# Attention of a decoder trunk: both key groups' scores in one step on alternating row halves, and sums over values with the values as weights

## The chip, the cores and the metric

The kernel runs on one core of a Trainium2 chip. The metric is the device time of one launch in microseconds, the median of several runs. A core has five engines with queues of their own: TensorE (PE in the profile, with its weight loads as PEld), VectorE (DVE), ScalarE (ACT), GpSimdE (POOL), and SyncE (SP), which here only issues DMAs.

## What is computed

One step of a two-layer decoder on 304 columns: 16 learned tokens and 256 prompt tokens (columns 0 to 271, the prompt group) and 8 sequences of 4 new tokens (columns 272 to 303, the sample group). Per layer:

```python
proj = x @ w_in                      # q: 8 heads x 64, k, v: 2 key heads x 64; xr, gate, g_attn, g_lru: 1024 each
s = einsum(q, k) * HEAD_DIM ** -0.5  # window of 128 keys, masked with NEG_INF
m = maximum(s.max(-1), sink)
p = exp(s - m)
denom = p.sum(-1) + exp(sink - m)    # a learned sink of each head joins the sum
attn = einsum(p / denom, v)
rec = rg_lru(causal_conv(xr)) * gelu(gate)
mix = (sigmoid(g_attn) * (attn @ w_attn_proj) + sigmoid(g_lru) * (rec @ w_lru_proj)) @ w_out
x = layer_norm(alpha * x + mix)
x = layer_norm(alpha * x + swiglu(x))
```

All results are float32. The eight query heads share two key heads: heads 0 to 3 belong to group 0, heads 4 to 7 to group 1.

## The kernel before, in words

Columns are tokens, rows are channels, so that the result of a product is the moving operand of the next. Every large product is three float32r products of split parts (`wh`, `wl` are the two parts of a weight unit, `xh`, `xl` those of the activations): L363, L364 and L365, 24 of them for one tile of 128 output columns. Such a tile is one job, and a weight unit of eight 128 x 128 tiles feeds it. ACT and DVE split the weights (L212, L213) up to four units ahead.

The jobs of the first half of a layer are counted as steps: the q and k products up to step 6, then `ga`, `xr`, the rest of `ga`, `gate` and `gl`, up to step 37. The attention and the recurrence have no stretch of their own. A table `PLAN` names for each layer the step at which a piece of them is written into the program, between jobs or in the middle of one: `a0` and `ad` the first step and the spacing of attention steps, `c0` and `g0` those of the convolution and of the gates (`rg`), `r` the square roots, `p0` and `m0` the scan and what follows it. A scheduler then sets the order on each engine.

The attention of the prompt group has three blocks of queries: block 0, the 16 learned tokens (layer 0 only); block 1, the next 128 tokens, with 16 + 128 keys; block 2, the last 128, with 128 + 128 keys. A `Unit` is one block, one group `g` and two heads (four in block 0). So layer 0 has 2 + 4 + 4 units, layer 1 has 4 + 4; one `Sample` unit stands among them. A unit goes through four stages, some attention steps apart (`BEHIND`):

- `scores`: the mask goes into a bank `sc` as a bf16 product (L514), the products of q (weights, 64 rows: rows 0 to 63 for group 0, 64 to 127 for group 1) and keys add to it (L518), DVE takes the maximum (L522, L523), ACT the exponentials with their sums (L528) into `P`.
- `turn`: TensorE transposes `P`, key block by key block (L541), into `pt`, and ACT copies it to `PT` (L544, L547).
- `values`: for each head and key block a product with `PT` as weights (16 or 128 rows) and 64 columns of the values `vn` moving (L558) into a bank `o` of the whole block. After the block's last unit DVE divides by the denominators (L563 to L568) into `O`.
- `back`: `O` is transposed back (L580, `ot`) and split into `ath` and `atl` (L350, L351), which the products with `w_attn_proj` (`ap`) read after step 37.

`v_turn` brings the values into rows of keys at step 8 (L480 to L482). Tiles come from 51 slots and PSUM tiles from 8 banks, each in rotation, with their users' ends as the only waits. A float32 product shows in the trace as two records, each with a weight load of its own.

Of the kernel before, what the change touches and what calls it, by code (L numbers as in the profile page):

```python
# [35 lines left out]
    dict(a0=10, ad=1, c0=14, cd=1, g0=18, gd=0.75, r=23.5, p0=29.5, pd=1, m0=33.5, sx=21.5, vt=8),  # L36
    dict(a0=12, ad=1.75, c0=13.5, cd=1.5, g0=16.5, gd=1.25, r=26, p0=26, pd=2.25, m0=30, sx=9, vt=8),
# [4 lines left out]
NC = 2  # L42
HOOK = 4
BEHIND = ((0, 2, 3, 4), (0, 2, 4, 6))
# [14 lines left out]
def ffn_order():  # L59
    """The inner layer's pairs of columns, and the parts of its way back, each LAG pairs behind its last one."""  # L60
    order, due = [], {min(b + LAG, 22): (a, b) for a, b in FPARTS}
    for f in range(2, 23):
        if f in due:
            order.append(due[f])
        if f < 22:
            order.append(f)
    return order


def unit_list():  # L70
    """The units of 128 x 128 weight tiles in the order in which TensorE takes them."""
# [51 lines left out]
def trunk_kernel(ctx, tc, I, O):  # L123
# [100 lines left out]
    def ahead(u):  # L224
        """Split the units that come up to LA main units behind u."""
# [102 lines left out]
    class Split:  # L328
        """Activations as pairs of tiles, each in two float32r parts, which take their place when first used."""
# [16 lines left out]
    def split(parts, x, scale=None):  # L346
        """parts = x (times a scale of each row), in two parts that float32r holds."""
# [8 lines left out]
    def product(ps, n, u, i0, ks, xs, cs, start=True, stop=True):  # L356
        """ps[:, :n] += the tiles of unit u from i0 on, times those of xs."""
# [31 lines left out]
    def job(name, n, src, cs, ks=range(8), fills=()):  # L389
        """The product of one tile of columns; fills come between its halves."""  # L390
# [10 lines left out]
    def grouped(name, cols, src, between=None):  # L401
        """The products of four tiles of columns, with the contraction's tiles on the outside."""
# [21 lines left out]
    for l in range(DEPTH):  # L424
# [10 lines left out]
        vn = slot(nm("vn"), [128, 4, 128])  # L435
# [3 lines left out]
        def unfold(ps, n, ccs, out=None):  # L439
            """The product, with the spread and the shift of the LayerNorm before it."""  # L440
# [34 lines left out]
        def v_turn():  # L475
# [7 lines left out]
            pool.dma_start(O["wvp"][l], vn[:, 2, :])  # L483
            pool.dma_start(O["wvn"][l], vn[:32, 3, :])
# [4 lines left out]
        V0, V1, V2, VN = (vn[:, j, :] for j in range(4))  # L489
        BLK = {  # L490
            0: dict(q0=0, nq=16, keys=(0, 16), mask=mask0, v=((V0, 16),)),
            1: dict(q0=16, nq=128, keys=(0, 144), mask=mask1, v=((V0, 16), (V1, 128))),
            2: dict(q0=144, nq=128, keys=(16, 272), mask=mask2, v=((V1, 128), (V2, 128))),
        }
        blk_state = {}

        class Unit:
            """Scores of some heads of a block, from the products to the sum over the values."""

            def __init__(self, b, g, ts):  # L500
                self.b, self.g, self.ts = b, g, ts

            def scores(self):
                B = BLK[self.b]
                nq, (k0, k1), nt = B["nq"], B["keys"], len(self.ts)
                nk = k1 - k0
                if self.b not in blk_state:
                    blk_state[self.b] = dict(
                        nm=tiny("nm", 8), rs=tiny("rs", 8), left=8)
                S = blk_state[self.b]  # L510
                ps = bank(nm("sc"))
                w = 512 // nt
                p3 = ps[:nq, :].rearrange("p (a b) -> p a b", a=nt)[:, :, :nk]
                pe.matmul(p3, identb[:nq, :nq], B["mask"][:nq, None, :].to_broadcast([nq, nt, nk]),  # L514
                          start=True, stop=False, skip_group_check=True)
                gs = slice(64 * self.g, 64 * self.g + 64)
                for a, t in enumerate(self.ts):
                    pe.matmul(p3[:, a, :], qr[t // 2][gs, t % 2, B["q0"]:B["q0"] + nq], kr[gs, k0:k1],  # L518
                              start=False, stop=True, skip_group_check=True)
                c = slice(4 * self.g + self.ts[0], 4 * self.g + self.ts[0] + nt)  # L520
                mx = tiny("mx", 8)
                dve.tensor_reduce(mx[:nq, :nt], p3, axis=AX.X, op=OP.max)  # L522
                dve.scalar_tensor_tensor(S["nm"][:nq, c], mx[:nq, :nt], -0.125, nsink[:nq, l, c],  # L523
                                         op0=OP.mult, op1=OP.min)
                self.P = slot(nm("P"), [128, nt, nk])
                for a in range(nt):
                    h = c.start + a
                    act.activation(self.P[:nq, a, :], p3[:, a, :], AF.Exp, bias=S["nm"][:nq, h:h + 1],  # L528
                                   scale=0.125, accum_out=S["rs"][:nq, h:h + 1])

            def turn(self):
                B = BLK[self.b]
                nq, nt = B["nq"], len(self.ts)
                p = bank(nm("pt"))
                nv = len(B["v"])
                p4 = p[:, :nt * nv * nq].rearrange("p (a b c) -> p a b c", a=nv, b=nt)
                self.PT = slot(nm("PT"), [128, nv, nt, nq])
                for a in range(nt):
                    o = 0
                    for j, (_, n) in enumerate(B["v"]):  # L540
                        pe.transpose(p4[:n, j, a, :], self.P[:nq, a, o:o + n], identf[:nq, :nq])  # L541
                        o += n
                if all(n == 128 for _, n in B["v"]):
                    act.activation(self.PT, p4, AF.Copy)  # L544
                else:
                    for j, (_, n) in enumerate(B["v"]):
                        act.activation(self.PT[:n, j], p4[:n, j], AF.Copy)  # L547

            def values(self):
                B = BLK[self.b]  # L550
                S = blk_state[self.b]
                nq, nt = B["nq"], len(self.ts)
                if "o" not in S:
                    S["o"] = bank(nm("o"))
# [578 lines left out]
```

## Time and profile before

| | |
|---|---|
| median of three runs | 931.6 us (931.28 to 933.31) |
| profiled execution, span | 929.2 us |
| the median less the span | 2.4 us |
| TensorE busy | 906.0 us (98%) |
| DVE, ACT, POOL busy | 694.2, 507.4, 175.7 us |
| attention of layer 0 (40 to 130 us) | TensorE busy 90.0 of 90 us |
| attention of layer 1 (515 to 623 us) | TensorE busy 106.2 of 108 us |

Busy shares are counted from records that overlap: a 304-column product lasts 0.30 us by its record, but the next starts 0.14 us after it. So what an instruction costs TensorE is read from start to start: a group's cost is the start of what follows it less its own start. A timeline row merges equal records ("x8"); its second number reaches to the end of the last.

### The profile page before, as it was taken

Reading aid. Unit: us, or ns where it says so; the run is one execution under the profiler, and the core shown is the slowest. Engines: PE = TensorE matmul, PEld = TensorE weight load, DVE = VectorE, ACT = ScalarE, POOL = GpSimd, SP = SyncE. Lnnn points to the kernel's source line nnn. Section 1 sums busy time; section 2 is a strip of 40 time slices with the busy share of each in tenths; the row PEclk is TensorE's granted clock in tenths of the full one; section 3 lists DMA queues with packets and bytes.
Section 4 is the critical chain, followed back from the end, with each engine's and each line's share of the span. In section 5 each row is a group of like instructions: output and inputs, shape, how many; then the busy total and the mean of one; then the engine's idle time right before and its main releaser. Section 6 shows DMA issues by size and latency. Waiting matters only on the chain.

```text
span 929.2 us, 16206 instructions
## 1 busy us (share of the span) xinstructions
PE 906.0 (98%) x6520; PEld 885.0 (95%) x6520; DVE 694.2 (75%) x1153; ACT 507.4 (55%) x871; POOL 175.7 (19%) x242
## 2 busy tenths in 40 slices
PE   9999999999999999999997999999999999999994
PEld 7988999999999999999997998999999999999993
DVE  5756859567998567678899886685689985877865
ACT  4865894445565333444557876954456643444432
POOL 2910118023300000000342430130253000000025
PEclk9999999999999999999998999999999999999997
DMA  7743225444344443545463343155444544445401
GB/s 256 281 177 119 95 88 208 157 158 161 136 163 156 156 151 115 213 138 175 143 217 116 120 162 137 46 170 189 148 164 153 178 156 163 147 171 181 159 24 51
DMA packets 26347, 141.62 MB, mean 152 GB/s; under 512 B 3304, under 2 KB 7432, under 8 KB 11936
## 3 DMA queue, kind: packets, MB, share of 16 engines
q1 hardware_dynamic: 25280, 137.93, 42.7%
q0 software_dynamic: 992, 2.66, 0.9%
q8 instruction: 51, 0.84, 0.4%
q14 instruction: 24, 0.20, 0.1%
HBM read 136.74 MB, written 3.83 MB: 151 GB/s over the span
## 4 chain that ended last, share of the span: by engine, by line
PE 90%; DVE 4%; issue 2%; DMA 1%; POOL 1%; ACT 1%; SPq 0%; DVEq 0%; POOLq 0%; ACTq 0%
PE f L364 10%; PE f L363 10%; PE f L365 9%; PE rs L363 6%; PE rs L365 6%; PE rs L364 6%; PE xr L363 2%; PE xr L365 2%; PE xr L364 2%; PE gate L363 2%; PE rp L365 2%; PE gate L364 2%; PE o L558 2%; PE rp L363 2%; PE rp L364 2%; PE gate L365 2%
## 5 line engine op out<-in xcount | busy, mean ns | idle before, releaser
L212 ACT ACTIVATE wh<-raw 128x1024 fp32r<-128x1024 f32 (+2 forms) x255 | 262.8, 1032 | 238.3 <-PE rs L365 69.0
L213 DVE TENSOR_TENSOR wl<-raw,wh 128x1024 fp32r<-128x1024 f32 (+2 forms) x255 | 310.8, 1223 | 84.2 <-ACT wh L212 81.9
L364 PE MATMUL f<-dh,wl 128*128 128x306 f32 (+1 forms) x640 | 192.7, 301 | 0.0
L363 PE MATMUL f<-dh,wh 128*128 128x306 f32 (+1 forms) x640 | 192.3, 301 | 0.0
L365 PE MATMUL f<-dl,wh 128*128 128x306 f32 (+1 forms) x640 | 191.3, 299 | 0.0
L364 PEld LDWEIGHTS f<-dh,wl 128*128 128x128 f32 x640 | 121.1, 189 | 0.0
L365 PEld LDWEIGHTS f<-dl,wh 128*128 128x128 f32 x640 | 120.8, 189 | 0.0
L363 PEld LDWEIGHTS f<-dh,wh 128*128 128x128 f32 x640 | 120.5, 188 | 0.0
L363 PE MATMUL rs<-fh,wh 128*128 128x304 f32 (+1 forms) x352 | 105.5, 300 | 0.0
L364 PE MATMUL rs<-fh,wl 128*128 128x304 f32 (+1 forms) x352 | 105.0, 299 | 0.0
L365 PE MATMUL rs<-fl,wh 128*128 128x304 f32 (+1 forms) x352 | 104.8, 299 | 0.0
L923 POOL TENSOR_TENSOR acc<-acc,X 128x304 f32<-128x304 f32 (+1 forms) x23 | 29.7, 1289 | 359.6 <-ACT e L918 195.5
L363 PEld LDWEIGHTS rs<-fh,wh 128*128 128x128 f32 x352 | 66.2, 188 | 0.5 <-ACT fh L350 0.4
L364 PEld LDWEIGHTS rs<-fh,wl 128*128 128x128 f32 x352 | 66.1, 188 | 0.1
L365 PEld LDWEIGHTS rs<-fl,wh 128*128 128x128 f32 x352 | 66.1, 188 | 0.0
L874 DVE TENSOR_TENSOR X<-X,rs 128x304 f32<-128x304 f32 (+1 forms) x64 | 29.4, 460 | 32.4 <-PE rs L365 31.7
L363 PE MATMUL xr<-xh,wh 128*128 128x304 f32 x128 | 41.0, 320 | 3.8 <-ACT xh L801 3.8
L970 DVE SCALAR_TENSOR_TENSOR u<-c,c,f 128x304 f32<-128x304 f32 (+1 forms) x80 | 41.4, 520 | 1.8
L969 DVE COPY c<-f 128x2 f32<-128x2 f32 x80 | 12.5, 158 | 39.6 <-PE f L365 39.3
L365 PE MATMUL xr<-xl,wh 128*128 128x304 f32 x128 | 39.3, 310 | 1.5 <-DVE xl L803 1.5
L364 PE MATMUL xr<-xh,wl 128*128 128x304 f32 x128 | 39.5, 310 | 0.0
L363 PE MATMUL rs<-mgh,wh 128*128 128x304 f32 (+1 forms) x128 | 38.8, 303 | 0.0
(303 smaller groups left out, 2243.6 us busy)
## 6 DMA issues: line engine op xcount, KB each, us to landing
raw<-in_wts SPq DMA_DIRECT2D x112, 1024.0 KB, 4.8
raw<-in_wts SPq DMA_DIRECT2D x16, 768.0 KB, 4.3
raw<-in_wts SPq DMA_DIRECT2D x3, 512.0 KB, 8.5
kc<-in_kcache SPq DMA_DIRECT2D x4, 256.0 KB, 7.1
vc<-in_vcache SPq DMA_DIRECT2D x4, 256.0 KB, 7.2
out_wks<-kc POOLq DMA_DIRECT2D x4, 256.0 KB, 4.9
out_wvs<-vc POOLq DMA_DIRECT2D x4, 248.0 KB, 4.4
xt<-in_xT SPq DMA_DIRECT2D x3, 304.0 KB, 7.5
```

The source lines that it names most:

```text
L212: act.activation(hi[:, s], r, AF.Copy)
L213: (pool if u in LO_POOL else dve).tensor_sub(lo[:, s], r, hi[:, s].bitcast(F32))
L363: pe.matmul(ps[:, :n], hi[:, w], xh, start=first, stop=False)
L364: pe.matmul(ps[:, :n], lo[:, w], xh, start=False, stop=False)
L365: pe.matmul(ps[:, :n], hi[:, w], xl, start=False, stop=last)
L558: pe.matmul(o3[:, self.g, t, :], self.PT[:n, j, a, :], v[:n, 64 * self.g:64 * self.g + 64], start=j == 0, stop=j == len(B["v"]) - 1)
L874: dve.tensor_add(z, z, ps[:, :W])
L923: on("sum", l).tensor_add(self.sum, self.sum, z)
L969: dve.tensor_copy(c2[:, 2 * i:2 * i + 2], b[:, W:W + 2])
L970: dve.scalar_tensor_tensor(t1[:, i], off, c2[:, 2 * i + 1:2 * i + 2], b[:, :W], op0=OP.mult, op1=OP.add)
```

## The change

A unit now holds both groups, so layer 0 has 1 + 2 + 2 units and layer 1 2 + 2. `scores` fills two banks: both masks, then the products of the heads with the groups alternating (rows 0 to 63, rows 64 to 127, and so on). The denominators are formed here, from the maxima and the sums of this unit, and DVE multiplies `P` by their reciprocals before it is transposed (two multiplications of 288 or 512 elements a row); before, it divided the sum over the values, once for each block. `turn` makes the same number of transposes, now with the 16-row pieces after the 128-row ones, and copies those of both groups into one tile `F` (rows 0 to 15 and 32 to 47 of 48, the rest zeroed by POOL). `values` has the values as weights: `vz` holds for each key block and group a 128 x 128 tile with that group's 64 columns and zeros in the others; `v0` the first 16 keys of both groups. The moving operand is `PT`, 256 columns (two heads of 128 queries), and the products of both groups add up in one bank that is already transposed. So `back` and its transposes are gone for the prompt group, and the bank is split into `ath` and `atl` at once. In `v_turn` ACT makes five copies for three, and POOL zeroes `vz` and `v0` at the layer's start.

```diff
-    dict(a0=10, ad=1, c0=14, cd=1, g0=18, gd=0.75, r=23.5, p0=29.5, pd=1, m0=33.5, sx=21.5, vt=8),
-    dict(a0=12, ad=1.75, c0=13.5, cd=1.5, g0=16.5, gd=1.25, r=26, p0=26, pd=2.25, m0=30, sx=9, vt=8),
+    dict(a0=10, ad=2, c0=14, cd=1, g0=18, gd=0.75, r=23.5, p0=29.5, pd=1, m0=33.5, sx=21.5, vt=8),
+    dict(a0=12, ad=3.5, c0=13.5, cd=1.5, g0=16.5, gd=1.25, r=26, p0=26, pd=2.25, m0=30, sx=9, vt=8),
-BEHIND = ((0, 2, 3, 4), (0, 2, 4, 6))
+BEHIND = ((0, 3, 4, 5), (0, 4, 7, 9))
...
+        pool.memset(vz, 0.0)
+        pool.memset(v0[:, 0], 0.0)
...
-            act.activation(vn[:, 1:3, :], p3[:, 1:3, :], AF.Copy)
-            act.activation(vn[:16, 0, :], p3[:16, 0, :], AF.Copy)
-            act.activation(vn[:32, 3, :], p3[:32, 3, :], AF.Copy)
+            for g in range(2):
+                d = slice(64 * g, 64 * g + 64)
+                act.activation(vz[:, :, g, d], p3[:, 1:3, d], AF.Copy)
+                act.activation(v0[32 * g:32 * g + 16, 0, d], p3[:16, 0, d], AF.Copy)
+                pool.dma_start(O["wvp"][l][:, d], vz[:, 1, g, d])
+            act.activation(v0[:32, 1, :], p3[:32, 3, :], AF.Copy)
...
+                for p in p3:
+                    pe.matmul(p, identb[:nq, :nq], B["mask"][:nq, None, :].to_broadcast([nq, nt, nk]),
+                              start=True, stop=False, skip_group_check=True)
                 for a, t in enumerate(self.ts):
+                    for g in range(2):
+                        gs = slice(64 * g, 64 * g + 64)
+                        pe.matmul(p3[g][:, a, :], qr[t // 2][gs, t % 2, B["q0"]:B["q0"] + nq], kr[gs, k0:k1],
+                                  start=False, stop=True, skip_group_check=True)
...
+                dve.tensor_add(es, es, rs)
+                dve.reciprocal(rec, es)
+                for g in range(2):
+                    P = self.P[g][:nq]
+                    dve.tensor_mul(P, P, rec[:, g, :, None].to_broadcast([nq, nt, nk]))
...
+                if nf:
+                    self.F = slot(nm("PF"), [128, n])
+                    pool.memset(self.F[:48], 0.0)
...
-                for a, t in enumerate(self.ts):
-                    for j, (v, n) in enumerate(B["v"]):
-                        pe.matmul(o3[:, self.g, t, :], self.PT[:n, j, a, :], v[:n, 64 * self.g:64 * self.g + 64],
-                                  start=j == 0, stop=j == len(B["v"]) - 1)
+                todo = [(vz[:, v, g, :], self.PT[g][:, j]) for j, v in enumerate(B["v"]) for g in range(2)]
+                if B["first"]:
+                    todo.append((v0[:48, 0, :], self.F[:48]))
+                for i, (v, x) in enumerate(todo):
+                    pe.matmul(o, v, x, start=i == 0, stop=i == len(todo) - 1)
...
-            def back(self):
...
+        au = [Unit(1, (0, 1)), Unit(1, (2, 3)), Unit(2, (0, 1)), Unit(2, (2, 3))]
+        if l == 0:
+            au.insert(0, Unit(0, (0, 1, 2, 3)))
+        au.insert(2, Sample())
```

The first place is TensorE in layer 0, where the attention passes from block 1 to block 2. Before, one program piece between two jobs holds the sums over values of a unit of block 1 (`o`), the transposes of the next one (`pt`) and the scores of a unit of block 2 (`sc`, the mask first); `rg` is a product of the gates:

```order
L643 MATMUL sot_1143<-identf,sO_1083 128x128 x2
L558 MATMUL o_939<-vn_192,PT_1086 128x64 x4
L541 MATMUL pt_1158<-identf,P_1023 16x128
L541 MATMUL pt_1158<-identf,P_1023 128x128
...
L514 MATMUL sc_1166<-mask_109,identb 128x512
L518 MATMUL sc_1166<-kr_190,qr_188 128x256 x2
L712 MATMUL rg_1179<-xch_882,lwh_886 128x328
```

In the changed kernel the transposes of a unit of block 1 stand one step (24 products of jobs and six of `rg`) ahead of its sums over values; those come as three products, and the scores of a unit of block 2 follow with both masks ahead and the groups taking turns:

```order
L574 MATMUL o_1296<-PT_1235,vz_192 128x256
L516 LDWEIGHTS identb
L516 MATMUL sc_1302<-mask_109,identb 128x512
L574 MATMUL o_1296<-PT_1243,vz_192 128x256
L574 MATMUL o_1296<-PF_1227,v_22_193 128x256
L516 LDWEIGHTS identb
L516 MATMUL sc_1303<-mask_109,identb 128x512
L521 MATMUL sc_1302<-kr_190,qr_189 128x256
L521 MATMUL sc_1303<-kr_190,qr_189 128x256
```

What moved: four products of 64 columns for one group became three of 256 columns for both, and the scores of two groups, which stood a step apart, stand together.

The second place is ACT at the start of layer 1, where it makes the parts `xh` of the next input tile by tile (L801 before, L791 after) and TensorE waits for them. Before, nothing of the attention's values stands there (the copies to `vn` come 15 rows later):

```order
L801 ACTIVATE xh_5472<-X_327,cvec 128x304 x2
L212 ACTIVATE wh_5681<-raw_5381 128x1024
L590 ACTIVATE qblk<-qr_5260 64x2x8x4
L801 ACTIVATE xh_5484<-X_329,cvec 128x304 x2
L590 ACTIVATE qblk<-qr_5260 64x2x8x4
L801 ACTIVATE xh_5496<-X_331,cvec 128x304 x2
```

After, the five copies of `v_turn` stand between the second and the third pair of tiles (`v_681` is `v0`):

```order
L791 ACTIVATE xh_5440<-X_330,cvec 128x304 x2
L485 ACTIVATE vz_5229<-vT_5637 128x2x64
L486 ACTIVATE v_681_5230<-vT_5637 16x64
L485 ACTIVATE vz_5229<-vT_5637 128x2x64
L486 ACTIVATE v_681_5230<-vT_5637 16x64
L488 ACTIVATE v_681_5230<-vT_5637 32x128
L212 ACTIVATE wh_5652<-raw_5349 128x1024
L791 ACTIVATE xh_5452<-X_332,cvec 128x304 x2
```

The third pair of `xh` has moved behind five more copies on ACT.

## Rows read from the trace of the kernel before

**Rows 1.** The page: busy time of each engine, and the chain's shares by engine
```profile
PE 906.0 (98%) x6520; PEld 885.0 (95%) x6520; DVE 694.2 (75%) x1153; ACT 507.4 (55%) x871; POOL 175.7 (19%) x242
PE 90%; DVE 4%; issue 2%; DMA 1%; POOL 1%; ACT 1%; SPq 0%; DVEq 0%; POOLq 0%; ACTq 0%
```
**Rows 2.** Waits of PE over the span: us in total, times, longest
```profile
PE xr L363 <- ACT xh L801: 3.8, 1, 3.8
PE ot L580 <- DVE O L568: 1.8, 1, 1.8
PE xr L365 <- DVE xl L803: 1.5, 1, 1.5
```
**Rows 3.** Stretches: us, busy of PE, PEld, DVE, ACT, POOL, PEclk, DMA
```profile
40.00:130.00 90.00, 90.00 (x665) 82.33 (x664) 58.49 (x119) 65.00 (x170) 15.97 (x34) 1.00 0.38 132
...
515.00:623.00 108.00, 106.18 (x779) 99.26 (x778) 80.55 (x152) 84.94 (x179) 29.36 (x40) 1.00 0.38 130
```
**Rows 4.** Timeline of PE, block 1 in layer 0: start, us, line, out<-in, shape, count
```profile
67.93 0.29 PE L514 MATMUL sc<-mask,identb 128*128 128x288 bf16 x1
68.15 0.75 PE L518 MATMUL sc<-kr,qr 64*128 64x144 f32 x4
68.83 0.41 PE L363 MATMUL xr<-xh,wh 128*128 128x304 f32 x1
...
93.67 0.30 PE L365 MATMUL ga<-xl,wh 128*128 128x304 f32 x1
93.90 1.52 PE L558 MATMUL o<-vn,PT 16*128 16x64 f32 x8
95.26 0.60 PE L541 MATMUL pt<-identf,P 128*128 128x128 f32 x4
```
**Rows 5.** Timeline of PE, block 2 in layer 0: scores, sums, transposes back
```profile
95.70 0.38 PE L514 MATMUL sc<-mask,identb 128*128 128x512 bf16 x1
96.01 1.13 PE L518 MATMUL sc<-kr,qr 64*128 64x256 f32 x4
97.07 0.41 PE L363 MATMUL ga<-xh,wh 128*128 128x304 f32 x1
...
120.89 1.00 PE L558 MATMUL o<-vn,PT 128*128 128x64 f32 x8
121.69 0.40 PE L712 MATMUL rg<-xch,lwh 128*128 128x328 f32 x1
...
126.05 0.60 PE L580 MATMUL ot<-identf,O 128*128 128x128 f32 x4
126.40 0.39 PE L363 MATMUL gate<-xh,wh 128*128 128x304 f32 x1
```
**Rows 6.** Timeline of PE: the Sample unit's scores, on four strips of 32 columns
```profile
61.77 0.64 PE L601 MATMUL ss<-kc,qblk 128*32 128x128 f32 x16
62.35 0.41 PE L363 MATMUL xr<-xh,wh 128*128 128x304 f32 x1
```
**Rows 7.** Groups by form on DVE: shape, count, busy us, mean ns, idle before
```profile
L568 DVE TENSOR_TENSOR O<-o,es 128x512 f32<-128x512 f32 x4 | 2.8, 690 | 2.0 <-PE o L558 2.0
L458 DVE TENSOR_TENSOR sw<-sw,rope 128x288 f32<-128x288 f32 x4 | 1.8, 452 | 1.6 <-ACT sw L456 1.6
```
**Rows 8.** Groups by form on ACT and DVE: exponentials, copies, maxima
```profile
L528 ACT ACTIVATE P<-sc,nm 128x256 f32<-128x256 f32 x16 | 7.4, 469 | 3.3 <-DVE nm L523 3.3
L547 ACT ACTIVATE PT<-pt 16x256 f32<-16x256 f32 x8 | 2.9, 360 | 1.6 <-PE pt L541 1.6
L522 DVE TENSOR_REDUCE mx<-sc 128x2 f32<-128x512 f32 x8 | 5.5, 690 | 8.0 <-PE sc L518 8.0
```
**Rows 9.** Timeline of ACT at the start of layer 1: the parts of the input
```profile
502.12 0.25 ACT L590 ACTIVATE qblk<-qr 64x64 f32<-64x64 f32 x1
502.38 1.18 ACT L801 ACTIVATE xh<-X,cvec 128x304 fp32r<-128x304 f32 x2
```
**Rows 10.** Timeline of DVE there: last in-place scale of that input
```profile
504.72 0.43 DVE L802 TENSOR_SCALAR X<-X,cvec 128x304 f32<-128x304 f32 x1
```

More of the change, by code (lines that the diff above doesn't have):

```diff
@@ L488, in trunk_kernel @@
         attn = Split("at", T)
-        V0, V1, V2, VN = (vn[:, j, :] for j in range(4))
+        VN = v0[:, 1, :]
         BLK = {
-            0: dict(q0=0, nq=16, keys=(0, 16), mask=mask0, v=((V0, 16),)),
-            1: dict(q0=16, nq=128, keys=(0, 144), mask=mask1, v=((V0, 16), (V1, 128))),
-            2: dict(q0=144, nq=128, keys=(16, 272), mask=mask2, v=((V1, 128), (V2, 128))),
+            0: dict(q0=0, nq=16, keys=(0, 16), mask=mask0, first=True, v=()),
+            1: dict(q0=16, nq=128, keys=(0, 144), mask=mask1, first=True, v=(0,)),
+            2: dict(q0=144, nq=128, keys=(16, 272), mask=mask2, first=False, v=(0, 1)),
@@ L494, in trunk_kernel, with __init__ @@
         }
[L495 removed]
         class Unit:
[L500 to L501 removed]
+            stages = ("scores", "turn", "values")
+            def __init__(self, b, ts):
+                self.B, self.ts, self.nt = BLK[b], ts, len(ts)
             def scores(self):
[L504 to L505 removed]
+                B, nt = self.B, self.nt
+                nq, (k0, k1) = B["nq"], B["keys"]
@@ L506, in scores @@
                 nk = k1 - k0
[L507 to L515, printed above, removed]
@@ L525, in scores @@
[L525 to L529, printed above, removed]
-            def turn(self):
[L532 to L547, printed above, removed]
@@ new lines, in values @@
+            def values(self):
+                B, nt = self.B, self.nt
+                nq, q0 = B["nq"], B["q0"]
+                o = bank(nm("o"))[:, :nt * nq]
+                todo = [(vz[:, v, g, :], self.PT[g][:, j]) for j, v in enumerate(B["v"]) for g in range(2)]
[3 more added lines that the diff above has]
+                    pe.matmul(o, v, x, start=i == 0, stop=i == len(todo) - 1)
+                o = o.rearrange("p (a b) -> p a b", a=nt)
+                for i in range(0, nt, 2):
+                    split([x[:, :, q0:q0 + nq] for x in attn.pair(self.ts[i] // 2)], o[:, i:i + 2])
@@ L585, in trunk_kernel @@
         class Sample:
+            stages = ("scores", "turn", "values", "back")
             def scores(self):
@@ L648, in back @@
                         split([x[gs, :, NP:].rearrange("p t (b s) -> p t b s", b=NB) for x in attn.pair(j)], src)
-        au = []
-        for b in ((0, 1, 2) if l == 0 else (1, 2)):
-            for ts in (((0, 1, 2, 3),) if b == 0 else ((0, 1), (2, 3))):
-                for g in range(2):
-                    au.append(Unit(b, g, ts))
-        au.insert(4, Sample())
-        stages = ("scores", "turn", "values", "back")
-        def attn_step(i):
-            for d, stage in reversed(list(zip(BEHIND[l], stages))):
-                if 0 <= i - d < len(au):
-                    getattr(au[i - d], stage)()
+        au = [Unit(1, (0, 1)), Unit(1, (2, 3)), Unit(2, (0, 1)), Unit(2, (2, 3))]
+        if l == 0:
+            au.insert(0, Unit(0, (0, 1, 2, 3)))
+        au.insert(2, Sample())
         ext, xc, ta, tb, tv, gel = {}, {}, {}, {}, {}, {}
@@ L783, in trunk_kernel @@
         at(P["vt"], v_turn)
-        for i in range(len(au) + BEHIND[l][3]):
-            at(P["a0"] + i * P["ad"], attn_step, i)
+        steps = [(P["a0"] + i * P["ad"] + d, -n, getattr(u, x))
+                 for i, u in enumerate(au) for n, (d, x) in enumerate(zip(BEHIND[l], u.stages))]
+        for s, _, f in sorted(steps, key=lambda e: e[:2]):
+            at(s, f)
         for t in range(8):
```

74 lines of the change are left out of this document (36 added, 38 removed).

## The prediction

> **What bounds the kernel now.** I first read the busy times and the chain. TensorE is busy in 906.0 of 929.2 us and holds 90% of the chain of work that ended last [rows 1]. Then I read its waits: the longest are 3.8 us for `xh` and 1.5 us for `xl`, both where layer 1 begins, and 1.8 us at `ot`, which waits for the division on DVE [rows 2]. Third, the stretches: in layer 0's attention TensorE is busy 90.00 of 90 us, in layer 1's 106.18 of 108, at a granted clock of 1.00 (2.4 GHz), while DVE has 65% and 75%, ACT 72% and 79% [rows 3]. So in the attention the queue of TensorE sets the time, and a microsecond off it is a microsecond off the kernel, as long as the others deliver. The change must therefore be costed from start to start on TensorE.
>
> A float32 product is two passes, two records. The four passes of 144 columns in a unit's scores take 68.15 to 68.83, .68 us [rows 4], those of 256 columns 96.01 to 97.07, 1.06 us [rows 5]. The difference, .38 us for 4 x 112 columns, is .83 ns a column: .12 us for a pass of 144 columns, .213 for one of 256. What is left over is .20 us (.68 - .48), which I take for the change of tile shape, from 64 rows back to 128. The mask ahead takes .22 us (67.93 to 68.15) in block 1 and .31 (95.70 to 96.01) in block 2, of which some .1 is that the next product, of another shape, doesn't overlap with it.
>
> **Part 1: the scores.** Before, two units (both groups of two heads) cost 2 x .90 = 1.80 us in block 1 [rows 4] and 2 x 1.37 = 2.74 in block 2 [rows 5]. The number of passes stays, but they alternate between rows 0 to 63 and 64 to 127 and go to different banks. Does TensorE run them at once? Before, the halves never stand together, so the trace bounds it from two sides. At one end they follow each other. At the other, the nearest thing: the Sample unit's products on four strips of 32 columns, 16 passes of 128 columns in .58 us (61.77 to 62.35) [rows 6]; in a row they would need 16 x .107 = 1.7. Less .20 for the shape, .38 us is just under four passes: all four strips work at once. I take the same for row halves, since it is the nearest row, so eight passes take four slots. A pair then costs, in block 1, .12 + .22 + .20 + 4 x .12 = 1.02 (the first mask without the change of shape), a gain of .78; in block 2, .21 + .31 + .20 + 4 x .213 = 1.57, a gain of 1.17. There are four pairs of each in the two layers: 3.1 + 4.7 = 7.8 us. Block 0, small products, gives .4: one change of shape and one mask less. If the halves need five slots for eight passes (a lag of one), the gain is 1.3 less, 4 x (.12 + .213).
>
> The Trainium skill says in "TensorEngine Tiling (Array Packing)", Key Properties, that row tiles, too, load weights and multiply independently; [rows 6] agree for columns alone, and no row of before shows it for rows. By that page the four slots would stand.
>
> **Part 2: the sums over values.** Before, a unit of block 1 (16 and 128 rows in turn) costs 1.45 us: 93.90 to 95.26, and .09 because the product ahead of it has .23 instead of the usual .14 to itself [rows 4]. A pair is 2.90. After: two products of 128 rows and one with `F`, 256 columns each: 4 x .213 for the first two, and for `F`, 48 rows, 2 x .213 + .20 + .10 = .73 if it counts as another shape. In all 1.58, a gain of 1.32, four times, 5.3 us. If 48 rows cost no change of shape, the four pairs gain 6.5; if such a pass takes longer than I think, 4.9. Block 2 gains nothing: a pair was 2 x .80 = 1.60 (120.89 to 121.69) [rows 5] and is now 8 x .213 = 1.71, since half of each weight tile is zeros: +.11, four times, .4 us lost. Block 0 gives .7 (16 short passes become two). The transposes `pt` stay in number and I cost their new order at nothing.
>
> **Part 3: the way back.** The five groups `ot` are gone, .35 us each (126.05 to 126.40) [rows 5]: 1.7 us. With them goes the division and so the wait of 1.8 us at `ot` [rows 2]. What is late there next is the last unit's `ath` and `atl`, but the work that fills the jobs until the products with `w_attn_proj` lies some steps behind it, so I let all of the 1.8 go.
>
> **Part 4: what moves to DVE, ACT and POOL.** DVE loses five divisions of .69 us and gains eight multiplications of 288 elements (a like one takes .452) and eight of 512 (.690) [rows 7]: 8 x .452 + 8 x .690 - 5 x .69 = 5.7 us, with the small operations on rows about 6.3 in two layers; its share goes to some 69% and 78% by that, to 75% and 84% if those multiplications turn out twice as long. ACT has the same exponentials (.469) and copies of the same size (.360 for a narrow one) [rows 8]. All of it lies beside TensorE's work unless a chain gets too long. Two chains do come close:
>
> From `turn` to `values` in layer 0 there is now one step, 24 products of .14 and six of the gates, about 4.3 us; before it was the same step, but then a unit had one or two copies, now it has four (block 1: two narrow, two wide, about 1.5 us), behind whatever stands in ACT's queue: `ath` copies that wait for their bank, weights, `xch`. I expect TensorE to wait .5 us at the first unit of block 1 and 1.0 at the second. Two score banks are held at a time until their exponentials are done, out of eight banks in rotation: .5. Together 2.0 us. The bounds are 0 (the next row of this kind, [rows 2], shows no such wait) and some 6.
>
> At the start of layer 1, ACT now makes the five copies of `v_turn` ahead of the third pair of `xh`. TensorE waits there for exactly these: a pair takes 1.18 us after a small copy of .25 [rows 9], and DVE, which follows with `xl` and the scaling in place, ends its last part at 505.15, 1.6 us behind the last `xh` on ACT [rows 9, 10]. Five copies are 1.0 to 1.25 us, but DVE lags ACT by about 1 us and swallows some: .4. POOL's zeroing of `vz` and `v0` shares that time: .4. Together .8, between 0 and 2.
>
> **The sum.** Gains: scores 7.8 + .4, values 5.3 - .4 + .7, way back 1.7 + 1.8, in all 17.3. Costs 2.0 + .8 = 2.8. Net 14.5 us: span 929.2 - 14.5 = 914.7, and with the 2.4 us that the median lies above it 917.1 us.
>
> **Rivals.** (B) The row halves do not run at once. Then a pair of scores saves only changes of shape and part of a mask, .30 or .32 us, 2.5 in all instead of 7.8, and block 0 .2 instead of .4: 5.5 less, 922.6 us. For it: nothing before shows halves together. Against it: the strips [rows 6]. Chance .14.
>
> (C) TensorE is ahead, and waits for the evacuation. If ACT's queue makes each of nine units late by some .7 us more than I put, the waits are 8 instead of 2 and the time is 923.1. For it: ACT at 79% and DVE at 75% in layer 1's attention [rows 3], now with less time for more work. Against it: neither makes TensorE wait there before, but for the 1.8 us. Chance .17. The Trainium skill warns of it in "TensorEngine Tiling (Array Packing)", PSUM Bottleneck: tiling speeds up TensorE, not the way out of PSUM. The waits of before give no sign of that inside the attention.
>
> (D) Slower than before. `P` must now be normalised before it is transposed, so a chain stands between scores and `pt` on TensorE's path: two maxima of .69, four exponentials of .47, two multiplications of .69 in block 2 [rows 7, 8], 4.6 us, with hops and small operations 6.5. `turn` comes three steps (layer 0, at least 11.5 us) or four (16 us) behind. If the queues of DVE and ACT stretch the chain by more than that, TensorE stops at `pt` of every unit, its place in nine units. The change is slower once that costs more than 17.3 / 9 = 1.9 us a unit, that is, from a chain of 13.4 us in layer 0; at 2.5 us it gives 22.5 lost, 936.8. DVE's 65 to 75% [rows 3] speak against a doubling. Chance .05.
>
> **How the numbers follow.** The forecast, row halves at once and small waits, has .57; without any new wait 914.3, with `F` at no cost of shape 913.1; five slots instead of four 918.4. B has .14 at 922.6, C .17 at 923.1, D .05, and better than 913 has .07. The forecast's range of 913 to 920 with B and most of C gives 913.0 to 923.0, which leaves about .2 out. All but D and the worst end of C are faster by far more than 0.2%, which is about what a measurement of this kernel can tell from no change: faster .93, same .02, slower .05.
>
> **What would show it.** In the trace of the changed kernel: two `sc` products with starts some 10 ns apart (else B), a pair of scores from mask to next job in 1.0 and 1.6 us, the `F` product in some .7, no `ot` and no wait for a division. TensorE's waits at `pt` (for `P`), at `o` (for `PT` or `PF`) and at `sc` (for a bank) should sum to about 2 us, else C or D. Layer 1's first waits, 5.3 us in all [rows 2], should grow by less than 1. I would be wrong most easily in the size of the waits, which rest on an order and not on a row, and in the halves.

## The result, and the profile after

The changed kernel takes 922.05 us (median of four runs, 920.84 to 924.32) against 931.76; the ratio is 0.9893 (0.9879 to 0.9907). In a second set on another occasion it took 924.25 (924.02 to 925.29), 0.9918 (0.9903 to 0.9933). So it is faster by about 1%, 8 to 10 us, where 14.5 were forecast: on the forecast side, 5 us short of the forecast in the first set and 6 in the second. The first median lies inside the forecast's range of 913 to 923 by one microsecond, the second just outside it. Its profiled execution has a span of 922.6 us, 6.6 less than that of before. It is the slowest of the first four, so the terms below are set against its own 6.6.

The page, and the first of TensorE's waits (us in total, times, longest), to be held against [rows 1, 2]:

```profile
PE 891.0 (97%) x6414; PEld 870.9 (94%) x6414; DVE 700.5 (76%) x1169; ACT 504.2 (55%) x876; POOL 185.4 (20%) x253
```
```profile
PE xr L363 <- ACT xh L791: 3.9, 1, 3.9
PE g L415 <- ACT xh L350: 3.7, 2, 2.8
PE so L627 <- ACT sPT L621: 2.9, 1, 2.9
PE o L574 <- ACT PT L563: 2.0, 3, 1.1
PE xr L365 <- DVE xl L793: 1.6, 1, 1.6
PE rg L700 <- ACT xch L350: 1.5, 1, 1.5
...
PE xr L363 <- DVE tg L760: 1.0, 1, 1.0
```

TensorE's records are 15 us shorter in sum, about the gain forecast, but the span is only 6.6 shorter: the rest is new waits. The wait at `ot` is gone; new are `so` for `sPT` (the Sample unit, layer 0), three at `o` (layer 0), `rg` for `xch` and `xr` for `tg` (layer 1). Those for `xh` and `xl` at layer 1's start are what they were, 3.9 and 1.6 for 3.8 and 1.5. The wait at `g` is the start of the kernel; it varies from .4 to 3.7 us between the profiles shown here, whatever the kernel.

Where the time went is told best by the two attention stretches, from the first product of `xr` to the first of `ap` (starts on TensorE's timeline, us; it stands here for all kernels of this study):

| kernel | layer 0 | layer 1 | median of runs |
|---|---|---|---|
| before | 137.9 | 137.1 | 931.76 |
| changed | 137.9 | 130.6 | 922.05 |
| changed, again (g2_again) | 138.0 | 130.4 | 924.25 |
| e1_so_later | 135.2 | 130.2 | 921.47 |
| e2_halves_apart | 141.3 | 130.3 | 925.79 |
| e3_all_later | 132.9 | 130.7 | 917.00 |
| g3_sample_turn | 134.5 | 129.7 | 920.76 |
| e4_turn_early | 130.0 | 130.1 | 916.39 |
| f1_mask_between | 132.9 | 133.0 | 923.65 |
| f2_old_values | 134.7 | 134.6 | 925.15 |
| f3_layer1 | 131.2 | 128.0 | 915.17 |
| f4_l1g | 130.4 | 129.1 | 916.06 |
| g1_clean | 129.2 | 128.7 | 914.96 |
| g4_clean_loops | 129.5 | 128.8 | 915.98 |

Layer 1 gained 6.5 us. Layer 0 gained nothing at all: with the same products made cheaper, it takes the same 137.9 us.

**The products themselves** came out nearly as forecast. TensorE's timeline of the changed kernel (start, us, line, operation, out<-in, shape, count; a cost is the next start less the group's own), a pair of scores and the sums of a unit in block 1, then the same of block 2:

```profile
529.58 0.42 PE L516 MATMUL sc<-mask,identb 128*128 128x288 bf16 x2
529.93 0.76 PE L521 MATMUL sc<-kr,qr 64*128 64x144 f32 x8
530.62 0.41 PE L363 MATMUL xr<-xh,wh 128*128 128x304 f32 x1
...
544.65 1.03 PE L574 MATMUL o<-PT,vz 128*128 128x256 f32 x4
545.61 0.70 PE L574 MATMUL o<-PF,v 48*128 48x256 f32 x2
546.24 0.31 PE L591 MATMUL ss<-masks,identb 128*128 128x320 bf16 x1
...
563.87 0.61 PE L516 MATMUL sc<-mask,identb 128*128 128x512 bf16 x2
564.41 1.13 PE L521 MATMUL sc<-kr,qr 64*128 64x256 f32 x8
565.47 0.42 PE L700 MATMUL rg<-xch,lwh 128*128 128x328 f32 x1
...
596.86 1.89 PE L574 MATMUL o<-PT,vz 128*128 128x256 f32 x8
598.40 0.48 PE L363 MATMUL gate<-xh,wh 128*128 128x288 f32 x1
```

Eight passes of scores take .69 us (529.93 to 530.62), as long as four did, .68 [rows 4]: the row halves work at once, and in four slots; the first two of the eight start 7 ns apart. A pair costs 1.04 and 1.60 us (forecast 1.02 and 1.57), the sums 1.59 in block 1 (1.58) and 1.54 in block 2 (1.71).

**What ate layer 0's gain** stands between 75 and 90 us. ACT's timeline (the bracket is its idle time before, and what ended it), then TensorE's there:

```profile
75.78 1.06 ACT L212 ACTIVATE wh<-raw 128x1024 fp32r<-128x1024 f32 x1 [0.65 <-PE ga L365]
77.58 0.48 ACT L350 ACTIVATE xch<-xc 128x328 fp32r<-128x328 f32 x1 [0.73 <-DVE xc L685]
79.57 1.06 ACT L212 ACTIVATE wh<-raw 128x1024 fp32r<-128x1024 f32 x1 [1.51 <-PE ga L365]
80.53 0.61 ACT L212 ACTIVATE lwh<-raw 128x512 fp32r<-128x512 f32 x1
81.06 0.46 ACT L350 ACTIVATE xch<-xc 128x328 fp32r<-128x328 f32 x1
81.42 0.40 ACT L755 ACTIVATE tg<-ga 128x304 f32<-128x304 f32 x1
81.72 0.37 ACT L620 ACTIVATE sPT<-spt 128x256 f32<-128x256 f32 x1
81.99 0.36 ACT L621 ACTIVATE sPT<-spt 32x256 f32<-32x256 f32 x1
```
```profile
75.85 0.27 PE L619 MATMUL spt<-identf,sP 128*32 128x128 f32 x1
...
82.40 1.17 PE L627 MATMUL so<-v,sPT 32*128 32x128 f32 x4 [2.91 <-ACT sPT L621]
```

The transposes `spt` end at about 76.1. Their two copies are made at 81.72 and 81.99, .7 us of work, and in between ACT is idle for 2.2 us (.73 and 1.51) behind the split of `xc`, whose input DVE has not made yet, and that of a weight unit, whose place a product of `ga` still reads. So the copies were late by their place in ACT's queue, not by ACT's load. The Trainium skill calls the queues of ScalarE and VectorE strict first in, first out ("TensorE: Matmul & The Clock Gate", Architectural detail); the trace agrees, ACT waiting 1.51 us for a weight split's place with a copy behind it that was ready.

Then the clock. Stretches (us, busy of PE, PEld, DVE, ACT, POOL, granted clock, DMA):

```profile
40.00:130.00 90.00, 85.13 (x603) 76.79 (x602) 62.46 (x128) 65.67 (x176) 23.06 (x38) 0.96 0.38 131
```
```profile
80.00:83.00 3.00, 0.60 (x3) 0.60 (x4) 2.27 (x4) 2.65 (x7) 0.00 (x0) 0.91 0.74 262
83.00:86.00 3.00, 3.00 (x23) 1.50 (x24) 0.42 (x1) 0.00 (x0) 0.00 (x0) 0.50 0.80 257
86.00:88.00 2.00, 2.00 (x10) 1.20 (x7) 0.41 (x1) 0.00 (x0) 0.00 (x0) 0.50 0.33 139
88.00:90.00 2.00, 2.00 (x12) 2.00 (x10) 1.21 (x4) 0.84 (x4) 0.00 (x0) 0.67 0.00 0
```

After the wait the granted clock is .50 (1.2 GHz), until about 89.3. In full-clock time that is 3 x .09 + 3 x .50 + 2 x .50 + 2 x .33 = 3.4 us lost, more than the wait itself. Before, the same stretch ran at 1.00 with TensorE always busy [rows 3].

**The account of 6.6 us.** Gains, from start to start over all groups of both layers: scores 8.1 (4 x (1.80 - 1.04) + 4 x (2.74 - 1.60) + .5 for block 0), sums over values 6.1 (4 x 1.31 + 4 x .06 + .7), way back 1.9 and its wait 1.8, transposes `pt` .5; 18.4 in all. Losses: waits of 2.9 + 2.0 in layer 0 and 1.5 + 1.0 in layer 1, 7.4; the clock 3.4; and the start of the kernel, where the first product of `q` comes at 22.2 instead of 21.7, .5; 11.3 in all. That leaves 7.1, for 6.6 measured. Taken from the two stretches instead, each less the idle time of TensorE and the clock lost in it (before 0 and 3.4 + 3.4, changed 4.9 + 3.4 and 4.0 + 3.4), the products gain 8.3 + 7.2, and 17.3 with the wait at `ot`: the two ways of counting differ by about 1 us.

### The profile page after: what moved, and what is told of

It is laid out like the page before. It is cut to its first block, busy times and chain, and to the rows that moved or that the text cites. A ratio compares the mean times of both kernels' runs of the same rounds, so it can differ in the third digit from the quotient of the medians.

```text
span 922.6 us, 16033 instructions
## 1 busy us (share of the span) xinstructions
PE 891.0 (97%) x6414; PEld 870.9 (94%) x6414; DVE 700.5 (76%) x1169; ACT 504.2 (55%) x876; POOL 185.4 (20%) x253
## 4 chain that ended last, share of the span: by engine, by line
PE 83%; DVE 4%; ACT 2%; issue 1%; POOL 0%; DVEq 0%; ACTq 0%
PE f L364 10%; PE f L363 10%; PE f L365 10%; PE rs L365 7%; PE rs L363 7%; PE rs L364 7%; PE gate L363 2%; PE gl L363 2%; PE rp L363 2%; PE gate L364 2%; PE rp L365 2%; PE gl L364 2%; PE rp L364 2%; PE gate L365 2%; PE gl L365 2%; PE o L574 1%
## 5 line engine op out<-in xcount | busy, mean ns | idle before, releaser
L363 PE MATMUL gate<-xh,wh 128*128 128x304 f32 (+1 forms) x128 | 39.2, 306 | 0.0
```

The lines of the kernel that those rows point to most:

```text
L363: pe.matmul(ps[:, :n], hi[:, w], xh, start=first, stop=False)
```

## The experiments

**Do the waits carry the loss?** Four kernels move stages of layer 0 apart, by one line each:

```diff
 e1_so_later:    the Sample unit alone
-zip(BEHIND[l], u.stages)
+zip((0, 3, 5, 6) if l == 0 and len(u.stages) == 4 else BEHIND[l], u.stages)
 e3_all_later:   every unit of layer 0
-BEHIND = ((0, 3, 4, 5), (0, 4, 7, 9))
+BEHIND = ((0, 3, 5, 6), (0, 4, 7, 9))
 e4_turn_early:  every unit of layer 0
+BEHIND = ((0, 2, 4, 5), (0, 4, 7, 9))
 g3_sample_turn: the Sample unit alone
+zip((0, 2, 4, 5) if l == 0 and len(u.stages) == 4 else BEHIND[l], u.stages)
```

> The Sample unit of layer 0 takes its sums over values one attention step (two counted steps... one of the table's) later, 5 instead of 4 behind its scores; nothing else is changed. Theory 1: layer 0 lost its gain to copies that ACT makes too late; the wait of 3.1 us at so for sPT and the half clock from 82.4 to about 88.7 us (3.1 us lost) go together, so the time falls by about 6 us, to 916, and the granted clock is 1.00 from 75 to 95 us. Theory 2: the wait only stands where some other engine is late in any case (DVE, or the weights), so it comes back at the next product that needs it, and the time stays within 2 us of 922.

Measured: 921.47 us (ratio to before 0.9884, 0.9865 to 0.9903), nearly nothing. The wait at `so`, 2.9 us by its row above (3.1 in the expectation), is gone, and one of the same size stands at `sot`, again with half the clock behind it. TensorE's wait, a stretch, and what ended just ahead of `sot` (it starts at 95.00) on DVE and ACT, of e1_so_later:

```profile
PE sot L639 <- ACT PT L563: 3.1, 1, 3.1
```
```profile
95.00:98.00 3.00, 3.00 (x8) 1.89 (x9) 2.26 (x5) 2.38 (x8) 0.54 (x1) 0.50 0.76 268
```
```profile
94.44 0.41 DVE L634 TENSOR_TENSOR sO<-so,sw 128x256 f32<-128x256 f32 x1
94.59 0.36 ACT L563 ACTIVATE PT<-pt 128x256 f32<-128x256 f32 x1
```

So theory 2 holds for this edit: the wait passed to the next stage of the same unit. Two things were late there together: the copy `PT`, which the wait is put down to and which ends at 94.95, and the division into `sO`, which DVE ends at 94.85, behind the convolution and two weight splits. Layer 0 is 2.7 us shorter all the same: two waits at `o` (.9 in all) are gone, and the half clock cost 1.7 us, not 3.4.

> The changed kernel with one thing moved: in layer 0 the Sample unit's transposes come two steps behind its scores instead of three, its sums over values stay. In ACT's order the two copies to sPT then stand ahead of the weights and of xch that they waited behind. If that order made the wait at so, the wait and the half clock behind it go, 6.2 us less than the profiled run, about 916.5 to 918, with the waits at o (1.2, .5, .7 us) still there. If ACT's load made it, the wait comes back at sot or o as in e1_so_later, and the time stays at 921 to 922.

Measured: 920.76 us (0.9876, 0.9847 to 0.9905; the runs spread from 917.0 to 923.5). `sPT` is in time, and the next `o` is late, by 2.3 us, with the clock at .50 behind it:

```profile
PE o L574 <- ACT PT L563: 3.3, 2, 2.3
```
```profile
98.00:101.00 3.00, 3.00 (x11) 1.74 (x12) 2.66 (x4) 1.02 (x2) 0.24 (x1) 0.50 0.52 218
```

My expectation of 916.5 to 918 failed. Putting one copy in its place does not help while the next stands one step behind its transposes too.

> All units of layer 0 take their sums over values two of the table's steps behind the transposes instead of one. Theory 1: the waits at o (1.2, .5 and .7 us) and at so (3.1) and the half clock (3.1) all go: 8.6 us less than the profiled run of the changed kernel, 914. Theory 2: the waits move on with the products, and the time stays above 919. If only e1 gains, the waits at o are made by something other than the copies' lateness.

Measured: 917.00 us (0.984, 0.9823 to 0.9857). All waits at `o` and `so` are gone, as theory 1 says; one remains at `sot`, whose distance to `so` is still one step, with a granted clock of .52 from 93 to 96 us behind it:

```profile
PE sot L639 <- DVE sO L634: 2.2, 1, 2.2
```

> Layer 0's transposes of P two steps behind the scores instead of three, sums over values where they are. It gives the copies the same two steps as the run before, and takes the step from the chain of maxima, exponentials and multiplications, which in the profile of the changed kernel took 5 us (72.1 to 77.0) of block 1. Theory 1: two steps are 8 us, the chain fits, so this too gives 914 to 916 and no wait at pt. If the chain is what bounds layer 0 (my rival D), TensorE waits at pt by 1 to 3 us a unit and the time is 922 or more.

Measured: 916.39 us (0.9833, 0.9818 to 0.9848). In layer 0 no wait at `o`, `so` or `sot`, and no fall of the clock; only .8 us at the first `pt`. Wait, and stretch:

```profile
PE pt L558 <- DVE P L540: 0.8, 1, 0.8
```
```profile
40.00:130.00 90.00, 89.18 (x660) 82.91 (x659) 65.84 (x137) 70.97 (x184) 20.55 (x37) 1.00 0.39 132
```

Layer 0 falls from 137.9 to 130.0 us. This settles two things. ACT is busier in the same 90 us (71.0 for 65.7) and DVE too (65.8 for 62.5), so their load was not what made TensorE wait; the step between `turn` and `values` was too short for four copies in queues that stop for other inputs. And the longer chain to `P` is no limit: two steps are enough, but for block 0. Why `sO` is late in e3 and in time here, both one step from `so`, is a matter of what stands around it on DVE; I did not take that apart.

**Are the concurrent halves worth what the sum says?** First the loops of the scores were exchanged:

```diff
-for a, t in enumerate(self.ts):
-    for g in range(2):
+for g in range(2):
+    for a, t in enumerate(self.ts):
```

> The changed kernel with the two loops of the scores exchanged: all products of rows 0 to 63, then all of rows 64 to 127. Count, masks and order of everything else stay. If the row halves work at once when they alternate, a pair of block 1 goes from 1.04 to 1.5 us and one of block 2 from 1.57 to 2.4, 5.3 us more over both layers: 927.4. If they do not, the time stays at 922. A part of a longer queue of TensorE can be taken up by the waits of layer 0, so 925 is still the first case.

Measured: 925.79 us (0.9935, 0.992 to 0.9949), 3.7 more, which by its number looks like the halves' price. It is not. TensorE's timeline of e2_halves_apart:

```profile
532.07 0.42 PE L516 MATMUL sc<-mask,identb 128*128 128x288 bf16 x2
532.42 0.77 PE L521 MATMUL sc<-kr,qr 64*128 64x144 f32 x8
533.12 0.41 PE L363 MATMUL xr<-xh,wh 128*128 128x304 f32 x1
```

The pair still costs 1.05 us, and layer 1 takes 130.3 us as before (130.6). The 3.4 us more are all in layer 0, where the wait at the second `o` has grown to 1.6 us and the clock falls a second time. So this run measured waits, not halves; the halves had not been parted. The exchange was tried again without waits, on g1_clean (below):

> g1_clean with the scores' loops exchanged, as in e2: all products of rows 0 to 63, then all of rows 64 to 127. If TensorE takes the second half's products ahead of their turn whatever the order, the time is that of g1_clean within 1 us, and the 3.7 us that e2 was slower by were waits and the clock. If the order counts, 916 or more.

Measured: 915.98 us (0.9825, 0.9811 to 0.984) beside 914.96 of g1_clean: the same within their spread, and 129.5 and 128.8 us in the two stretches for 129.2 and 128.7. The alternation itself is worth nothing; that both halves stand next to each other is what counts.

To part them, something that takes the whole array must stand between, and the second mask does (on e4_turn_early):

```diff
-for p in p3:
+for g, p in enumerate(p3):
     pe.matmul(p, identb, mask ...)
-for a, t in enumerate(self.ts):
-    for g in range(2):
+    for a, t in enumerate(self.ts):
         pe.matmul(p3[g][:, a, :], ...)
```

> From here on the base is e4_turn_early (916.4), whose layer 0 has next to no waits. In the scores the second group's mask, which takes the whole array, now stands between the products of rows 0 to 63 and those of rows 64 to 127, so the halves cannot meet; counts stay. Before this, exchanging the loops alone (e2) left the cost of a pair at 1.04 and 1.57 us, with starts 12 ns apart, so TensorE takes the other half's products ahead of their turn and that run did not part the halves. If the concurrent halves are worth what the prediction says, a pair costs 1.80 and 2.74 us, 4 x .78 + 4 x 1.17 + .4 = 8.2 more: 924.6. If the gain of the scores came from something else (fewer changes between jobs and scores), 917 to 919.

Measured: 923.65 us (0.989, 0.9867 to 0.9914), 7.3 more than e4_turn_early. Its timeline:

```profile
526.09 0.30 PE L516 MATMUL sc<-mask,identb 128*128 128x288 bf16 x1
526.32 0.75 PE L520 MATMUL sc<-kr,qr 64*128 64x144 f32 x4
527.01 0.30 PE L516 MATMUL sc<-mask,identb 128*128 128x288 bf16 x1
527.23 0.75 PE L520 MATMUL sc<-kr,qr 64*128 64x144 f32 x4
527.92 0.41 PE L363 MATMUL xr<-xh,wh 128*128 128x304 f32 x1
```

A pair costs 1.83 us for 1.04 (and 2.76 for 1.60 in block 2); over both layers 4 x .79 + 4 x 1.16 + .4 = 8.2 us, as expected. The stretches grow by less, 2.9 each, 5.8, mostly because waits took in a part: the one at `pt` (.8 before) is gone, the one for `tg` shrinks from 1.0 to .2 and the one for `xl` from 1.5 to 1.2. Less idle time and lost clock they are 7.8 longer; the last .4 stays open. Another 1.4 of the 7.3 us stand, in the profiled execution, at the start of the kernel (first product of `q` at 23.8 for 22.4), so that the time fits the expectation partly by luck. Nor is all of the 8.2 the concurrency itself: four more passes are .48 of the .79 and .85 of the 1.16, 5.3 in all; the rest is a second change of shape and a second mask by itself, which rival B would have saved too.

**What are the values as weights worth?** Only `values` and the way back were undone (on e4_turn_early):

```diff
-todo = [(vz[:, v, g, :], self.PT[g][:, j]) for j, v in enumerate(B["v"]) for g in range(2)]
-if B["first"]:
-    todo.append((v0[:48, 0, :], self.F[:48]))
-for i, (v, x) in enumerate(todo):
-    pe.matmul(o, v, x, ...)
+for a, t in enumerate(self.ts):
+    for g in range(2):
+        todo = [(self.F[:48, c], v0[:48, 0, d])] if B["first"] else []
+        todo += [(self.PT[g][:, j, c], vz[:, v, g, d]) for j, v in enumerate(B["v"])]
+        for i, (x, v) in enumerate(todo):
+            pe.matmul(o3[:, g, t, :], x, v, ...)
+... after the block's last unit: dve.tensor_copy(O, o3)
+def back(self): transposes of O into ot, split into ath and atl
```

> e4_turn_early with the sums over values as before: P, already normalised and transposed, as weights, 64 columns of the values moving, a bank for a block, a copy on DVE and the transposes back (ot). Only the first 16 keys differ from before: their weights have 48 rows, not 16. By the prediction's terms 5.3 - .4 + .7 for the sums and 1.7 for the way back come again, 7.3 us, and 1.8 for the wait at the last ot if it returns: 923.7 to 925.5. If the gain of the changed kernel is the scores alone, 918.

Measured: 925.15 us (0.9913, 0.9882 to 0.9943); the median is 8.8 above e4_turn_early, the span of the profiled execution 7.6. The first and the last row of a unit's sums in block 1, what follows them, and a stretch:

```profile
559.64 0.43 PE L579 MATMUL o<-v,PF 48*128 48x64 f32 x2
...
562.18 0.43 PE L579 MATMUL o<-vz,PT 128*128 128x64 f32 x2
562.45 0.38 PE L516 MATMUL sc<-mask,identb 128*128 128x512 bf16 x1
```
```profile
543.00:547.00 4.00, 4.00 (x28) 3.80 (x19) 2.70 (x7) 1.79 (x7) 0.00 (x0) 0.57 0.75 262
```

A unit's sums cost 2.81 us in block 1 (559.64 to 562.45) for 1.59. By the costs from start to start all sums take 19.5 us instead of 13.1 and `ot` 1.8, together 8.2. The two stretches are 4.7 and 4.5 us longer, 9.2. In that are .4 more wait at `pt` and a second fall of the clock in layer 1, which no other run has, 1.7 us (4 x .43), with TensorE at work throughout; at layer 1's start, on the other hand, .3 less was waited and .6 less lost to the clock. Less all idle time and lost clock the stretches are 8.0 longer. So both parts of the change are worth about 8 us each: the scores by the halves standing together, the values by their form and the way back that it saves.

**Layer 1's waits, and a better version.** Three kernels move numbers of layer 1's table on top of e4_turn_early, the last one also block 0's transposes:

```diff
-dict(a0=12, ad=3.5, c0=13.5, cd=1.5, g0=16.5, ...)
+dict(a0=12.5, ad=3.5, c0=13.5, cd=1.5, g0=17, ...)     f3_layer1
+dict(a0=12, ad=3.5, c0=13, cd=1.5, g0=17, ...)         f4_l1g
+dict(a0=12.5, ad=3.5, c0=13, cd=1.5, g0=17, ...)       g1_clean, with
+zip((0, 3, 4) if l == 0 and i == 0 else BEHIND[l], u.stages)
```

> e4_turn_early with two numbers of layer 1's table moved by half a step: attention from 12.5 instead of 12, gates from 17 instead of 16.5. Layer 1 has two waits that the kernel before has not: 1.0 us at xr for tg (a bank, at 510.7) and 1.5 us at rg for xch (at 566.2). If they are a matter of half a step, both go: 913.9. If the queues of DVE and ACT are simply too long there, they move on with the work, and the time stays at 916 to 917.

Measured: 915.17 us (0.98, 0.9772 to 0.9828). Layer 1 falls from 130.1 to 128.0 us, the wait for `tg` is gone, that for `xch` down to .3: half a step was the matter. The time gains only 1.2, as the wait at block 0's `pt` came out at 1.9 us there, with nothing changed in that place.

> As f3_layer1, but the attention stays at 12, the convolution comes half a step earlier (13) and the gates half a step later (17), so that xch has a whole step more. The wait for xch goes (1.5 us), the one for tg stays: 914.9. If xch's wait stays too, ACT's order sets it and not the distance.

Measured: 916.06 us (0.9805, 0.9782 to 0.9827). The wait for `xch` is gone, the one for `tg` (1.0) stays: the waits are as expected, layer 1 takes 129.1. On the median it is .3 better, less than such a measurement can tell.

> e4_turn_early with every wait moved away that the attention still has: block 0's transposes three steps behind its scores again (pt for P), layer 1's attention from 12.5, its convolution from 13, its gates from 17. If the price of the change is waits alone, it takes the .96 us at pt, 1.0 for tg and 1.5 for xch off 916.4: 912.8, and what is left against the kernel before is the bare sum of the products, 18 to 19 us. If one wait only passes its place to another, 914.5 or more.

Measured: 914.96 us (913.39 to 917.13; 0.9824, 0.9801 to 0.9847), in one set with the changed kernel's 924.25: 1% faster than that and 1.8% than before. Against e4_turn_early's 916.39 it is 1.4 better, which two medians here can hardly tell from nothing. It missed the 912.8 by a wait that has passed on, as the second case said: 1.9 us at a `ga`, for a bank that a copy `PT` still reads, in layer 1. Wait, and layer 0's stretch:

```profile
PE ga L363 <- ACT PT L563: 1.9, 1, 1.9
```
```profile
40.00:130.00 90.00, 89.97 (x665) 83.67 (x664) 66.63 (x136) 71.71 (x185) 23.50 (x38) 1.00 0.38 132
```

Its stretches are 8.7 and 8.4 us shorter than before's; with the 1.9 that makes 19.0. But part of that is the clock. At layer 1's start TensorE waits 3.7 to 3.8 us in both kernels, and the half clock behind it lasts half as long here. Stretches of before, then of g1_clean (its clock is 1.00 on either side):

```profile
498.00:501.00 3.00, 1.47 (x6) 1.47 (x7) 3.00 (x8) 3.00 (x6) 0.91 (x1) 0.51 0.72 300
501.00:505.00 4.00, 4.00 (x18) 4.00 (x18) 4.00 (x11) 2.52 (x6) 0.00 (x0) 0.52 0.59 205
```
```profile
490.00:494.00 4.00, 3.00 (x12) 3.00 (x13) 4.00 (x12) 3.96 (x11) 2.02 (x4) 0.57 0.47 193
```

That is 1.7 us lost (4 x .43) for 3.4 (3 x .49 + 4 x .48). Without this the gain is 17.3, as counted from the stretches of the changed kernel above: the gain of the products is there once TensorE doesn't wait.

> The changed kernel as it is, once more. Its four executions so far had mean clocks of .987 twice and .990 twice, and the two at .990 were 2.4 to 3.5 us shorter. If the half clock after the wait of 3.1 us at so does not come in every execution, a profile with .990 shows the same wait with a clock of 1.00 behind it, and ga to gate in layer 0 takes about 3 us less. If the clock always falls there, the difference comes from elsewhere (the input's loads at the start).

Measured: 924.25 us, with all four executions at mean clocks of .985 to .987. The profile shows the same waits (`so` 2.9, `o` 2.3, `rg` 1.5, `tg` 1.0) and the half clock again, so what the two faster executions of the first set did differently is not settled. The .003 by which their mean clocks differ are 2.8 us of 922, about the difference in time; where in the kernel it lies no profile shows. The kernel before has such a spread too: in that set its spans go from 928.5 us at a mean clock of .992 to 932.6 at .988. It is therefore no trait of the change, and differences under some 2 us between two medians here say little.

## Why the prediction was right, and where it was off

**The bound.** That TensorE's queue sets the time, and that start-to-start costs are the price, held: the sum made that way (17.3 us) came out at 18.4 counted by groups, at 17.3 counted from the stretches.

**Part 1, scores:** 8.2 forecast, 8.1 measured; f1_mask_between parts the halves, and its rows cost 8.2 more (7.8 in its stretches). Taking strips of columns as the nearest row for halves of rows was right. Row tiles, too, work at once, as I cited from the Trainium skill ("TensorEngine Tiling (Array Packing)", Key Properties); the .69 us for eight passes agree. Rival B is excluded.

**Part 2, values:** 5.6 forecast, 6.1 measured. `F` with 48 rows does count as another shape (.63 us, 545.61 to 546.24; .73 forecast). Block 2 gains .06 a pair instead of losing .11: its passes take .19 each, not .213.

**Part 3, way back:** 3.5 forecast, 3.7 measured, the wait at `ot` with it. `pt`, which I costed at nothing, gave .5, as the 16-row pieces stand together now.

**Part 4, new waits: the step that failed.** Forecast 2.0 in layer 0 and .8 at layer 1's start, 2.8; measured 10.8 in the profiled execution: 4.9 us of waits in layer 0, 2.5 in layer 1, 3.4 for the clock. The mechanism was named, a single step from `turn` to `values` with twice the copies in ACT's queue; three things about it were wrong. I counted only the units of block 1 and overlooked that the Sample unit's copies are in the same queue, where the longest wait came. I had no term for the clock that can fall behind a longer wait, though the trace of before shows it at layer 1's start: 3.8 us of wait [rows 2], then 7 us at .51 and .52. And layer 1's waits came not at its start (+.2 us, for .8) but at a bank and at `xch`, which I had not looked at.

**The rivals.** C comes closest, in kind and nearly by its time (923.1): TensorE ahead of what it is fed, 7.4 us of waits for its 8. But it spread them over nine units and gave ACT's and DVE's load as the reason; measured were 2.0 at three `o`, 2.9 at the Sample unit and 2.5 at `xch` and a bank, and the load was not the reason (e4_turn_early). That the first median still lies in the forecast's range is owed to its upper end, which was set to take in most of C. C had .17; the forecast's own case, small waits, had .57 and came only with e4_turn_early and g1_clean, which lie at the 914 to 917 that were named for it. I put too little on C because the trace of before showed no such waits inside the attention. But here a full TensorE had hidden the lateness of the others, and cheaper products uncovered it. D did not come: two steps hold the chain (e4_turn_early).

## What to carry to other kernels

When work is taken off an engine that is always busy, price the waits that it will uncover: list who feeds it at the shortest distance, and count what else stands in that feeder's queue, waiting for inputs of its own. Widen the distance for all stages at once; moved one at a time, the wait passes to the next. A run whose time fits an expectation may do so for another reason (e2_halves_apart): look at the rows for the thing that was to be changed.

## What the runs showed of the hardware

Two products on different row halves, in different banks, run at once even when one half's four passes all stand ahead of the other's in the program: the eight passes of e2_halves_apart take .70 us, as with the halves alternating; four after four with a single pass of overlap would take seven slots of .12 and the change of shape, 1.04. The Trainium skill says that matmuls start in program order ("TensorE: Matmul & The Clock Gate", The mechanism); these rows speak against it for passes on different row tiles. A product that takes the whole array between them ends it: 1.38 us for the same eight passes in f1_mask_between (.69 + .69).

The clock fell to .50 after waits of 2.9, 3.1, 2.3 and 2.2 us (changed kernel, e1_so_later, g3_sample_turn, e3_all_later) and stayed at 1.00 after that of 1.9 us in g1_clean and those of 1.1 at `o`; after the one of 1.6 us in e2_halves_apart, which followed an earlier fall, it fell again. The length of a wait alone does not decide, though. After 2.8 us at a `g` at the start of the changed kernel the clock stayed at 1.00 (9 to 15 us); after 1.8 us in the same place of g3_sample_turn it was .58 from 12 to 15 us. And in f2_old_values it fell at 543.4 us, to .57 from 543 to 547, when TensorE had been busy in all of the 4 us before. What sets it off is therefore open here. What a fall cost, 3.4 us in the changed kernel, 1.7 in e1_so_later and in g3_sample_turn (3 x .03 + 3 x .50 + 3 x .04), was between half of the wait ahead of it and more than that wait.
